# Three 256-column matmuls into one set of PSUM columns, in place of one of 512 and one of 256, in the feature blocks of a float32 decoder layer

## The chip, the core and the metric

One core of a Trainium2 chip. The metric is the device time of one execution in microseconds (us), the median of three runs. All times below are in us unless they are marked ns.

## What is computed

A hybrid decoder layer over 256 tokens and 2048 features, in float32: a recurrence with gates and a sparse attention side by side, merged, then a gated feed-forward part (ConvFFN), each followed by a layer norm. Cut to what the change touches:

```python
h = x @ w_in                                   # 2048 -> 12368 features
xr, gr, q, k, v, qi, ki, wi, g_rnn, g_att = split(h)
y_rnn = rg_lru(conv4(xr), ...) * gelu(gr)
score = sum_h wi_h * relu(rope(qi_h) @ rope(ki).T)   # top 64 keys of a query
y_att = attention(rope(q), rope(k), v, top-64 of score)
merged = sigmoid(g_rnn) * y_rnn + sigmoid(g_att) * y_att
x = layer_norm(2**0.25 * x + merged @ w_out)
u = conv3(x @ w_up)                            # 2048 -> 11264 features
x = layer_norm(2**0.25 * x + (silu(u[:, :5632]) * u[:, 5632:]) @ w_down)
```

## The kernel before, in words

**Splitting.** Every float32 operand of a product is split into a high part (cast to the type float32r) and a low part (the rest), and a product is the sum of three: high by high, high by low and low by high. A weight tile of 128 x 2048 is loaded by SyncE (SP), ScalarE (ACT) casts its two halves into `hi` (L116), VectorE (DVE) subtracts to get `lo` (L119). There are two `hi` and two `lo` buffers for each of two tiles, so the half of a tile can be cast when the same half of the tile two before it has left TensorE (PE). Casts and subtractions have priority over other work in the scheduler that orders each engine's queue.

**Feature blocks** (`feature_block`, L161). A block makes 128 output features (on partitions) for all 256 tokens (free). The source, `xt` or later `x1t` in the same place, holds for each of 16 groups of 128 input features 256 columns of high parts and then 256 columns of low parts. For each of the 16 groups, a *step* of the block, PE runs two matmuls: L170, the high weights by all 512 columns, into all 512 columns of the PSUM tile `psb`; and L174, the low weights by the 256 high columns, into the right half of `psb`. So the left half holds high by high, and the right half both cross terms. In the last step the order of the two is turned round.

**Evacuation** (`evacuate`, L311). ACT copies the right half of `psb` to a tile `ev` (L313), and DVE adds the left half to it and writes the destination (L314).

**Order of the work.** One block after another is written in program order; `project` (L185) runs a block, what takes its result, and then whatever was put off for some blocks (`after`, `tick`). The 181 feature blocks are: one for the indexer's key (80 features), 8 for its queries (`qi`), 4 for keys (`k`), 16 for queries (`q`) and 16 for the attention gate (`ga`), 48 for the recurrence (`xr`, `gr`, `gn`), and 88 for ConvFFN (L667). The products for values, `w_out` and `w_down` (`psv`, `pso`, `psd`) work the other way round, with tokens on partitions and matmuls of 512 columns throughout (`token_half`, L197 to L201).

**What stands between blocks.** Behind a `qi` block come the indexer's scores of an earlier block (`logits`, L383); behind `q` blocks the attention of one head (`attend`, L452 to L456, five matmuls of 256 columns, and `turn`, L475); behind `xr` blocks `gates` (L555 to L557, six matmuls of 256 columns: three add up in one half of a PSUM tile, three in the other). `k` and `q` results go through the rotation `rope` (shuffle on DVE L330, then three operations on GpSimd (POOL) L331 to L333) before ACT casts them. After the fourth `gn` block of a group ACT takes a sigmoid (L600), POOL a product and a sum (L601, L603), and ACT casts the merged result (L604).

Of the kernel before, what the change touches and what calls it, by code (L numbers as in the profile page):

```python
# [9 lines left out]
F32 = mybir.dt.float32  # L10
# [4 lines left out]
P = 128  # L15
PRIO = 30
T = 256
D = 2048
KT = D // P
# [7 lines left out]
LRU_C = 8.0  # L27
# [7 lines left out]

# Column starts in w_in.
C_XR, C_GR, C_Q, C_K, C_V, C_QI, C_KI, C_GRNN, C_GATT = (
    0, 2048, 4096, 6144, 6656, 7168, 8192, 8272, 10320)

# Columns of the per-feature parameters.  # L40
O_CW, O_CB, O_BA, O_BI, O_LAM, O_G1, O_B1, O_FW, O_FB = (
    0, 64, 80, 96, 112, 128, 144, 160, 424)
N_PAR = 512
# Columns of the constants.
O_ID, O_CI, O_SI, O_PEN = 0, 128, 384, 640
# [4 lines left out]
def hybrid_layer(ctx, tc, x, xT, w_blk, w_ki, w_v, lru_w, par, w_o, w_u, w_d, lnrows, consts, rot, out):  # L50
    nc = tc.nc
# [5 lines left out]

    # ---------------------------------------------------------------- weights
    order = []
# [34 lines left out]
    done = {"load": 0, "split": 0}  # L94
# [42 lines left out]

    # Work that is to wait until some more weight tiles have gone through the tensor engine.
    later = []
# [19 lines left out]

    # Features on partitions, tokens free: columns 0..255 hi*hi, 256..511 the cross terms.  # L160
    def feature_block(key, src, m=P):  # L161
        halves = weights(key)
        ps = psum.tile([P, 512], F32, tag="b", name="psb", bufs=4)
        for k in range(KT):
            hi, lo = halves[k // 8]
            o = (k % 8) * m
            first, last = k == 0, k == KT - 1

            def high():
                nc.tensor.matmul(ps[:m, :], hi[:, o:o + m], src[:, k, :], start=first, stop=last,  # L170
                                 skip_group_check=True)

            def low():
                nc.tensor.matmul(ps[:m, T:], lo[:, o:o + m], src[:, k, :T], start=False, stop=False,  # L174
                                 skip_group_check=True)
            if last:
                low()
                high()
            else:
                high()  # L180
                low()
        return ps

    # A block, its evacuation and then whatever waited for it.
    def project(key, fn, src=None, m=P):  # L185
        fn(feature_block(key, xt if src is None else src, m))
        tick()

    # Tokens on partitions, 512 features free; src_hi/src_lo hold features on partitions.
    def token_half(halves, t, ps, k0, hi_at, lo_at, kn):  # L190
# [19 lines left out]

    # The last tiles of a product: the first 128 tokens go through all of them, then the others.
    def token_tiles_held(keys, pss, k0, src, pool, between):
# [13 lines left out]
    nsp = base.tile([P, KT], F32, name="nsp")  # L226
# [6 lines left out]

    # Layer norm of the 128 rows r, 512 columns after another; done(c) takes them.
    def norm(r, g, b, t, done):
# [28 lines left out]

    # ---------------------------------------------------------------- phase 1
    wide = pool("wide")
# [13 lines left out]
    for k0, k1 in zip(cuts, cuts[1:]):  # L280
        r = xraw[k0 // 8][:, k0 % 8 * T:(k0 % 8 + k1 - k0) * T]
# [4 lines left out]
        r = r.rearrange("p (k t) -> p k t", t=T)  # L286
# [7 lines left out]
    for s in range(4):  # L294
        r = raw[:, s * 512:(s + 1) * 512]
        nc.sync.dma_start(r, order[1][1][:, s * 512:(s + 1) * 512])
        hi, lo = (h[:, s % 2 * 512:(s % 2 + 1) * 512] for h in halves[s // 2])
# [13 lines left out]
    def evacuate(ps, dst, work, m=P):  # L311
        t = work.tile([P, T], F32, tag="ev", name="ev", bufs=3)
        nc.scalar.copy(t[:m], ps[:m, T:])  # L313
        nc.vector.tensor_add(dst, ps[:m, :T], t[:m])  # L314

# [3 lines left out]

    # ---- indexer  # L320
    # Scores and attention weights keep queries 128..255 against all keys in columns 0..255,
    # queries 0..127 against keys 0..127 in columns 256..383.
    W2 = T + P
# [86 lines left out]

    # ---- keys and values
    # The parts of a key block lie side by side: keys 0..127 high, low, keys 128..255 high, low.
    kx = pa.tile([P, KV, 2, 2, P], F32R, name="kx")
# [23 lines left out]

    # ---- attention, one group of query heads after another
    def got_q(ps, n, g, pth, ptl):
# [66 lines left out]

    # ---- RG-LRU, four blocks of features at a time
    phm = ExitStack()
# [5 lines left out]

    # nsp = -LRU_C * softplus(-lambda), log1p by its series in e / (2 + e).
    lam = parm[:, O_LAM:O_LAM + KT]
# [47 lines left out]
    def recur(j0, v):  # L564
        xc, rg, ig, aa, th = (v[s] for s in ("xc", "rg", "ig", "aa", "th"))
        for i in range(NB):
            nc.scalar.activation(th[:, i], rg[:, i], AF.Tanh, scale=nsp[:, j0 + i:j0 + i + 1])
        for i in range(NB):
            nc.scalar.activation(aa[:, i], rg[:, i], AF.Exp, scale=nsp[:, j0 + i:j0 + i + 1])
        # 1 - a^2 = -tanh(log a) * (1 + a^2)  # L570
        nc.scalar.activation(rg, aa, AF.Square)
        nc.vector.scalar_tensor_tensor(th, rg, 1.0, th, op0=ALU.add, op1=ALU.mult)
        nc.scalar.activation(th, th, AF.Sqrt, scale=-1.0)
        nc.vector.tensor_mul(ig, ig, xc)
        nc.vector.tensor_mul(ig, ig, th)
        for i in range(NB):
            nc.vector.tensor_tensor_scan(rg[:, i], aa[:, i], ig[:, i], 0.0, op0=ALU.mult, op1=ALU.add)
# [30 lines left out]

    # ---------------------------------------------------------------- w_out and the first norm
    pho = ExitStack()  # L610
# [46 lines left out]

    # ---------------------------------------------------------------- ConvFFN
    phf = ExitStack()
# [27 lines left out]

    # ---------------------------------------------------------------- w_down and the second norm
    phd = ExitStack()
# [29 lines left out]
def _constants():  # L719
    def angles(rd):  # L720
        half = rd // 2
        inv = np.power(THETA, -np.arange(half, dtype=np.float64) * 2.0 / rd).astype(np.float32)
        ang = np.arange(T, dtype=np.float32)[:, None] * inv[None, :]
        return np.cos(ang.astype(np.float64)).T, np.sin(ang.astype(np.float64)).T

    c = np.zeros((P, N_CONST), np.float32)
    c[:, O_ID:O_ID + P] = np.eye(P)
    cos, sin = angles(16)
    c[:, O_CI:O_CI + T] = 1.0
    for r in (0, 64):  # L730
        c[r:r + 8, O_CI:O_CI + T] = cos
        c[r + 8:r + 16, O_CI:O_CI + T] = cos
        c[r:r + 8, O_SI:O_SI + T] = -sin
        c[r + 8:r + 16, O_SI:O_SI + T] = sin
    cos, sin = angles(32)
    rot = np.zeros((32, 2 * T), np.float32)
    rot[:16, :T], rot[16:, :T] = cos, cos
    rot[:16, T:], rot[16:, T:] = -sin, sin
    # Queries 128..255 against all keys, then queries 0..127 against keys 0..127.
    q = np.arange(P)[:, None]  # L740
    c[:, O_PEN:O_PEN + T] = np.where(np.arange(T)[None, :] > q + P, CAUSAL_FILL, 0.0)
    c[:, O_PEN + T:O_PEN + T + P] = np.where(np.arange(P)[None, :] > q, CAUSAL_FILL, 0.0)
    return c, rot
# [62 lines left out]
```

## Time and profile before

| | |
|---|---|
| three runs | 1472.03, 1469.31, 1472.29; median 1472.03 |
| profiled execution: span from first to last instruction | 1469.3 |
| its own time: the run of that length | 1469.31 |
| PE busy | 1430.9 (97%), 7718 matmuls and as many weight loads |
| DVE, ACT, POOL busy | 1008.9 (69%), 760.5 (52%), 269.3 (18%) |
| share of feature-block matmuls in the chain that ended last | L170 44%, L174 22% |

How to read it: the span of the profiled execution is the time of the fastest of the three runs, and 2.7 below the median. A matmul's row says when it started and how long it took from end to end; matmuls overlap, so a row of 256 columns lasts 280 ns and the next starts 120 ns after it. What a matmul costs in a stream is therefore read from the starts of consecutive rows, not from durations or from the busy time. A weight load (PEld) has its own row, which overlaps the matmul before.

### The profile page before, as it was taken

The numbers are of one execution on the slowest core, as the hardware profiler recorded it, in microseconds if no ns is written. First come the engines' busy times: TensorE is split into PE (matmuls) and PEld (weight loads), VectorE is DVE, ScalarE is ACT, GpSimd is POOL, SyncE is SP. The second block draws the span as 40 slices with busy tenths as digits, with TensorE's granted clock in tenths as the row PEclk, the third lists the DMA queues.
The fourth block names the chain that finished last, engine by engine and source line by source line (L and its number), as shares of the span: only waits on it lengthen the run. The fifth ranks groups of instructions, "written<-read, shape, count | busy, mean of one in ns | idle before, by whom it ended". The sixth has DMA issues, their size and how long they took to land.

```text
span 1469.3 us, 19909 instructions
## 1 busy us (share of the span) xinstructions
PE 1430.9 (97%) x7718; PEld 1222.6 (83%) x7718; DVE 1008.9 (69%) x1462; ACT 760.5 (52%) x1068; POOL 269.3 (18%) x227
## 2 busy tenths in 40 slices
PE   7989999999999999999799999999999999999996
PEld 6868888888888888888688888888888888888885
DVE  5787766777777777665776777677767775545456
ACT  4444555568777777644344444444444444433342
POOL 3541122220020211110422112211221120000002
PEclk9999999999999999999899999999999999999998
DMA  7435544545545454576355555555555557555552
GB/s 270 161 135 192 180 142 168 186 164 194 203 155 215 143 201 152 192 300 215 143 190 183 183 190 190 183 182 191 189 185 182 191 188 272 206 207 198 190 199 86
DMA packets 42205, 275.41 MB, mean 187 GB/s; under 512 B 4576, under 2 KB 4832, under 8 KB 10240
## 3 DMA queue, kind: packets, MB, share of 16 engines
q1 hardware_dynamic: 42112, 274.16, 52.2%
q8 instruction: 60, 0.98, 0.3%
q14 instruction: 33, 0.27, 0.1%
HBM read 269.94 MB, written 4.19 MB: 187 GB/s over the span
## 4 chain that ended last, share of the span: by engine, by line
PE 91%; DVE 4%; POOL 2%; DMA 1%; issue 1%; ACT 0%; SPq 0%; ACTq 0%; POOLq 0%; DVEq 0%
PE psb L170 44%; PE psb L174 22%; PE psd L201 5%; PE psd L197 5%; PE psd L199 5%; PE pso L201 2%; PE pso L199 2%; PE pso L197 2%; DVE lo L119 1%; DMA cst<-in_consts 1%; POOL qf L333 0%; POOL sh L332 0%; DMA xraw<-in_xT 0%; DVE rg L247 0%; PE psv L199 0%
## 5 line engine op out<-in xcount | busy, mean ns | idle before, releaser
L170 PE MATMUL psb<-xt,hi 128*128 128x512 f32 (+1 forms) x2896 | 1022.7, 400 | 6.4 <-ACT hi L116 5.4
L119 DVE TENSOR_TENSOR lo<-raw,hi 128x1024 fp32r<-128x1024 f32 (+2 forms) x488 | 609.9, 1253 | 361.7 <-ACT hi L116 352.1
L174 PE MATMUL psb<-xt,lo 128*128 128x256 f32 (+1 forms) x2896 | 786.1, 282 | 1.5 <-DVE lo L119 1.3
L116 ACT CAST hi<-raw 128x1024 fp32r<-128x1024 f32 (+1 forms) x488 | 509.5, 1048 | 365.8 <-PE psd L201 126.9
L170 PEld LDWEIGHTS psb<-xt,hi 128*128 128x128 f32 (+1 forms) x2896 | 536.8, 188 | 125.2 <-ACT hi L116 5.4
L174 PEld LDWEIGHTS psb<-xt,lo 128*128 128x128 f32 (+1 forms) x2896 | 547.9, 189 | 18.8 <-DVE lo L119 3.5
L683 POOL TENSOR_TENSOR y<-y 128x256 f32<-128x256 f32 x44 | 68.1, 1549 | 383.8 <-DVE y L675 362.3
L197 PE MATMUL psd<-hi,fh 128*128 128x512 f32 x352 | 136.9, 389 | 0.0
L199 PE MATMUL psd<-lo,fh 128*128 128x512 f32 x352 | 136.9, 389 | 0.0
L201 PE MATMUL psd<-hi,fl 128*128 128x512 f32 x352 | 136.9, 389 | 0.0
L675 DVE SCALAR_TENSOR_TENSOR y<-u,parm,y 128x255 f32<-128x255 f32 (+1 forms) x176 | 85.1, 484 | 6.2
L199 PEld LDWEIGHTS psd<-lo,fh 128*128 128x128 f32 x352 | 66.1, 188 | 13.8
L201 PEld LDWEIGHTS psd<-hi,fl 128*128 128x128 f32 x352 | 66.1, 188 | 13.7
L197 PEld LDWEIGHTS psd<-hi,fh 128*128 128x128 f32 x352 | 66.1, 188 | 13.5
L313 ACT COPY ev<-psb 128x256 f32<-128x256 f32 (+1 forms) x181 | 65.6, 362 | 0.8 <-PE psb L170 0.8
L684 ACT CAST fh<-y 128x256 fp32r<-128x256 f32 x44 | 17.9, 407 | 90.8 <-POOL y L683 90.8
L238 POOL TENSOR_SCALAR rstd<-mv 128x1 f32<-128x1 f32 x4 | 3.1, 778 | 294.8 <-DVE mv L236 294.8
L199 PE MATMUL pso<-lo,mh 128*128 128x512 f32 x128 | 49.9, 390 | 0.0
L197 PE MATMUL pso<-hi,mh 128*128 128x512 f32 x128 | 49.9, 390 | 0.0
L201 PE MATMUL pso<-hi,ml 128*128 128x512 f32 x128 | 49.8, 389 | 0.0
L331 POOL TENSOR_TENSOR qf<-qf,rots 32x256 f32<-32x256 f32 x16 | 15.5, 971 | 151.6 <-DVE sh L330 151.6
L681 ACT ACTIVATE y<-y 128x256 f32<-128x256 f32 x44 | 18.4, 419 | 47.0 <-DVE y L675 47.0
(172 smaller groups left out, 1028.0 us busy)
## 6 DMA issues: line engine op xcount, KB each, us to landing
raw<-in_w_blk SPq DMA_DIRECT2D x91, 1024.0 KB, 4.8
raw<-in_w_u SPq DMA_DIRECT2D x88, 1024.0 KB, 4.7
raw<-in_w_d SPq DMA_DIRECT2D x44, 1024.0 KB, 4.7
raw<-in_w_o SPq DMA_DIRECT2D x16, 1024.0 KB, 4.8
raw<-in_w_v SPq DMA_DIRECT2D x4, 1024.0 KB, 4.8
lwr<-in_lru_w SPq DMA_DIRECT2D x4, 512.0 KB, 3.7
g<-in_lnrows SPq DMA_DIRECT2D x2, 1024.0 KB, 6.6
xres<-in_x SPq DMA_DIRECT2D x4, 512.0 KB, 7.3
```

The lines of the kernel that those rows point to most:

```text
L116: nc.scalar.copy(hi[:, :w], raw[:, s * w:(s + 1) * w])
L119: eng.tensor_sub(lo[:, o:o + step], raw[:, s * w + o:s * w + o + step], hi[:, o:o + step].bitcast(F32))
L170: nc.tensor.matmul(ps[:m, :], hi[:, o:o + m], src[:, k, :], start=first, stop=last, skip_group_check=True)
L174: nc.tensor.matmul(ps[:m, T:], lo[:, o:o + m], src[:, k, :T], start=False, stop=False, skip_group_check=True)
L197: nc.tensor.matmul(ps, hi_at(k, t), hi[:, o:o + 512], start=first, stop=False, skip_group_check=True)
L199: nc.tensor.matmul(ps, hi_at(k, t), lo[:, o:o + 512], start=False, stop=False, skip_group_check=True)
L201: nc.tensor.matmul(ps, lo_at(k, t), hi[:, o:o + 512], start=False, stop=last, skip_group_check=True)
L313: nc.scalar.copy(t[:m], ps[:m, T:])
L675: nc.vector.scalar_tensor_tensor(y[:, s:], u[:, :T - s], w(tap), y[:, s:], op0=ALU.mult, op1=ALU.add)
L681: nc.scalar.activation(yg, yg, AF.Silu)
L683: nc.gpsimd.tensor_mul(yg, yg, yu)
L684: nc.scalar.copy(fh[:, j], yg)
```

## The change

A step of a feature block becomes three matmuls of 256 columns, all of which add up in the left half of `psb`: high weights by high columns, high weights by low columns, low weights by high columns. Every step has the same order, the last too. The evacuation becomes one ACT copy of that half straight to the destination; the tile `ev` and the DVE addition are gone. The rest of the diff removes comments. Line numbers after L164 fall by 12, from L314 on by 14.

```diff
         for k in range(KT):
             hi, lo = halves[k // 8]
             o = (k % 8) * m
-            first, last = k == 0, k == KT - 1
-
-            def high():
-                nc.tensor.matmul(ps[:m, :], hi[:, o:o + m], src[:, k, :], start=first, stop=last,
-                                 skip_group_check=True)
-
-            def low():
-                nc.tensor.matmul(ps[:m, T:], lo[:, o:o + m], src[:, k, :T], start=False, stop=False,
-                                 skip_group_check=True)
-            if last:
-                low()
-                high()
-            else:
-                high()
-                low()
+            hi, lo = hi[:, o:o + m], lo[:, o:o + m]
+            for n, (w, x) in enumerate(((hi, src[:, k, :T]), (hi, src[:, k, T:]), (lo, src[:, k, :T]))):
+                nc.tensor.matmul(ps[:m, :T], w, x, start=k == 0 and n == 0, stop=k == KT - 1 and n == 2)
         return ps
...
     def evacuate(ps, dst, work, m=P):
-        t = work.tile([P, T], F32, tag="ev", name="ev", bufs=3)
-        nc.scalar.copy(t[:m], ps[:m, T:])
-        nc.vector.tensor_add(dst, ps[:m, :T], t[:m])
+        nc.scalar.copy(dst, ps[:m, :T])
```

On PE, the first half of the first `qi` block, before (`hi_0`, `lo_0` are the first halves of its weight tile):

```order
L170 MATMUL psb<-xt,hi_0_115 128x512
L174 MATMUL psb<-xt,lo_0_116 128x256
L170 MATMUL psb<-xt,hi_0_115 128x512
L174 MATMUL psb<-xt,lo_0_116 128x256
L170 MATMUL psb<-xt,hi_0_115 128x512
L174 MATMUL psb<-xt,lo_0_116 128x256
```

and the same place with the change (x2: two such rows one after the other):

```order
L169 MATMUL psb<-xt,hi_0_115 128x256 x2
L169 MATMUL psb<-xt,lo_0_116 128x256
L169 MATMUL psb<-xt,hi_0_115 128x256 x2
L169 MATMUL psb<-xt,lo_0_116 128x256
L169 MATMUL psb<-xt,hi_0_115 128x256 x2
L169 MATMUL psb<-xt,lo_0_116 128x256
```

Two matmuls of a step have become three, for the same 768 columns.

On ACT, where the recurrence's first group of four ends and the next begins, before (`hi_0`, `hi_1`: the halves of one weight tile; `gn`: the gate's results; `mh`: the cast merged result; the brackets say which engines the row waits for):

```order
L313 COPY ev<-psb 128x256
L116 CAST hi_0_4077<-raw_3922 128x1024 [waits DMAHW1_49,DVE_49,PE_49]
L600 ACT_TABLE_LOAD
L600 ACTIVATE gn<-gn 128x1024 [waits DVE_49]
L116 CAST hi_1_4081<-raw_3922 128x1024 [waits PE_49,Activation_49]
L313 COPY ev<-psb 128x256
L604 CAST mh<-gn 128x1024 [waits Pool_49]
L116 CAST hi_0_4130<-raw_3968 128x1024 [waits DMAHW2_49,PE_49,Activation_49]
```

and with the change:

```order
L300 COPY gn<-psb 128x256 [waits PE_49]
L586 ACT_TABLE_LOAD
L586 ACTIVATE gn<-gn 128x1024 [waits Activation_49]
L116 CAST hi_0_4889<-raw_4692 128x1024 [waits DMAHW1_49,DVE_49,PE_49]
L590 CAST mh<-gn 128x1024 [waits Pool_49]
L116 CAST hi_1_4893<-raw_4692 128x1024 [waits DVE_49,PE_49]
L300 COPY xr<-psb 128x256 [waits PE_49]
L116 CAST hi_0_4956<-raw_4752 128x1024 [waits DMAHW2_49,DVE_49,PE_49]
```

The sigmoid has moved ahead of the first cast of the tile, and the cast of `mh`, which waits for POOL, now stands ahead of the second half of that tile and of the copy of the first `xr` block.

## Rows read from the trace of the kernel before

**Rows 1.** The page: PE's busy time, and the chain that ended last by engine and by line.

```profile
PE 1430.9 (97%) x7718; PEld 1222.6 (83%) x7718; DVE 1008.9 (69%) x1462; ACT 760.5 (52%) x1068; POOL 269.3 (18%) x227
PE 91%; DVE 4%; POOL 2%; DMA 1%; issue 1%; ACT 0%; SPq 0%; ACTq 0%; POOLq 0%; DVEq 0%
```

**Rows 2.** The page's groups of instructions: the two matmuls of a step (busy us, mean ns of one, idle before them).

```profile
L170 PE MATMUL psb<-xt,hi 128*128 128x512 f32 (+1 forms) x2896 | 1022.7, 400 | 6.4 <-ACT hi L116 5.4
L174 PE MATMUL psb<-xt,lo 128*128 128x256 f32 (+1 forms) x2896 | 786.1, 282 | 1.5 <-DVE lo L119 1.3
```

**Rows 3.** The chain in order of time: the last matmul of a ConvFFN block, and of the block 84 blocks later (start, us).

```profile
737.34 0.47 PE psb L170 x2
...
1212.22 0.47 PE psb L170 x2
```

**Rows 4.** Timeline of PE around one group of gates: start, us, line, shape.

```profile
363.70 0.39 PE L170 MATMUL psb<-xt,hi 128*128 128x512 f32 x1
363.93 0.28 PE L555 MATMUL pg<-xh,lwh 128*128 128x256 f32 x1
364.04 0.28 PE L556 MATMUL pg<-xl,lwh 128*128 128x256 f32 x1
364.16 0.28 PE L557 MATMUL pg<-xh,lwl 128*128 128x256 f32 x1
...
364.52 0.28 PE L557 MATMUL pg<-xh,lwl 128*128 128x256 f32 x1
364.64 0.40 PE L170 MATMUL psb<-xt,hi 128*128 128x512 f32 x1
364.87 0.28 PE L174 MATMUL psb<-xt,lo 128*128 128x256 f32 x1
```

**Rows 5.** Timeline of PE at one attention head: the first of its five matmuls of 256 columns (L452 to L456), and the matmul behind the fifth.

```profile
141.28 0.28 PE L452 MATMUL ps_s<-kx,qh 128*128 128x256 f32 x1
...
141.88 0.39 PE L170 MATMUL psb<-xt,hi 128*128 128x512 f32 x1
```

**Rows 6.** Timeline of PE in w_down, where all matmuls have 512 columns: nine matmuls from the first row to the last.

```profile
1299.78 0.39 PE L199 MATMUL psd<-lo,fh 128*128 128x512 f32 x1
...
1301.82 0.39 PE L199 MATMUL psd<-lo,fh 128*128 128x512 f32 x1
```

**Rows 7.** The chain in order of time: two starts of L170, nine steps apart, in a `qi` block right behind the indexer's scores.

```profile
42.86 0.23 PE psb L170
...
45.98 0.23 PE psb L170
```

**Rows 8.** Weight loads at the same gates, and the loads of two matmuls that follow each other with the same weights in w_down (L197, L199).

```profile
363.93 0.19 PEld L556 LDWEIGHTS pg<-xl,lwh 128*128 128x128 f32 x1
364.05 0.19 PEld L557 LDWEIGHTS pg<-xh,lwl 128*128 128x128 f32 x1
...
L199 PEld LDWEIGHTS psd<-lo,fh 128*128 128x128 f32 x352 | 66.1, 188 | 13.8
L197 PEld LDWEIGHTS psd<-hi,fh 128*128 128x128 f32 x352 | 66.1, 188 | 13.5
```

**Rows 9.** Groups: the addition that goes, in ConvFFN, the copy that stays, and the subtraction that makes `lo`.

```profile
L314 DVE TENSOR_TENSOR u<-psb,ev 128x256 f32<-128x256 f32 x88 | 36.8, 418 | 0.0
L313 ACT COPY ev<-psb 128x256 f32<-128x256 f32 x180 | 65.2, 362 | 0.8 <-PE psb L170 0.8
...
L119 DVE TENSOR_TENSOR lo<-raw,hi 128x1024 fp32r<-128x1024 f32 (+2 forms) x488 | 609.9, 1253 | 361.7 <-ACT hi L116 352.1
```

**Rows 10.** Groups of PE by shape whose idle time another engine ended: values, indexer scores, gates.

```profile
L199 PE MATMUL psv<-lo,xt 128*128 128x512 f32 x32 | 13.5, 422 | 3.5 <-DVE lo L119 3.5
L556 PE MATMUL pg<-xl,lwh 128*128 128x256 f32 x32 | 9.3, 292 | 2.0 <-DVE xl L547 2.0
L555 PE MATMUL pg<-xh,lwh 128*128 128x256 f32 x32 | 9.3, 290 | 1.7 <-ACT xh L546 1.7
L383 PE MATMUL pl<-kih,qil 64*128 64x256 f32 x32 | 4.9, 300 | 0.9 <-POOL qil L372 0.9
```

**Rows 11.** Busy time by stretch, for the key blocks and the value product that follows: length, busy us (x instructions) of PE, PEld, DVE, ACT and POOL, then PE's granted clock as a share of full speed, the DMA share, and GB/s.

```profile
95.00:108.00 13.00, 9.21 (x40) 6.52 (x39) 11.14 (x34) 5.14 (x8) 3.63 (x4) 1.00 0.28 105
108.00:115.00 7.00, 7.00 (x24) 5.58 (x25) 7.00 (x25) 3.36 (x4) 2.14 (x3) 0.76 0.48 159
```

**Rows 12.** Timelines of ACT and POOL where the first group of the recurrence ends, and from the chain the end of the second block behind that group.

```profile
399.66 0.36 ACT L313 COPY ev<-psb 128x256 f32<-128x256 f32 x1
...
402.47 1.28 ACT L600 ACT_TABLE_LOAD   x1
403.76 1.06 ACT L600 ACTIVATE gn<-gn 128x1024 f32<-128x1024 f32 x1
...
410.67 1.05 ACT L604 CAST mh<-gn 128x1024 fp32r<-128x1024 f32 x1 [4.63 <-POOL gn L603]
...
404.90 2.40 POOL L601 TENSOR_TENSOR gn<-gn,rg 128x1024 f32<-128x1024 f32 x1 [20.12 <-ACT gn L600]
407.38 3.25 POOL L603 TENSOR_TENSOR gn<-gn,macc 128x1024 f32<-128x1024 f32 x1
...
409.73 0.47 PE psb L170 x2
```

## The prediction

> **What bounds the kernel now.** I read the page first. PE is busy 97% of the span, and 91% of the chain that ended last is PE [rows 1]. The two matmuls of a feature block's step are the costliest groups, 2896 steps in 181 blocks, and PE hardly idles ahead of them: 6.4 and 1.5 us in all [rows 2]. So the stream of matmuls sets the time, and the question is how far apart they start. Durations do not tell: a row of 256 columns lasts 282 ns [rows 2], yet starts come closer. From the end of one ConvFFN block to the end of the one 84 blocks later it is 1212.22 - 737.34 = 474.88 us [rows 3], so a block takes 5.653 us and a step, with 768 columns, 353.3 ns. Almost all blocks run so.
>
> Three other places show what a matmul costs in a stream. The clock is granted in full nearly everywhere, 1.00 in the first row of [rows 11], the level of 2.4 GHz, at which 512 columns last 213.3 ns and 256 last 106.7. In w_down nine matmuls of 512 columns take 1301.82 - 1299.78 = 2.04 us, 226.7 ns each [rows 6]: 13.3 over their columns. At an attention head five of 256 take 0.60 us, 120 ns each [rows 5]: again 13.3 over. Around the gates, two of 512 and six of 256 take 364.87 - 363.70 = 1.17 us; their 2560 columns are 1066.7 ns, which leaves 12.9 ns for each of the eight [rows 4]. One price fits all three: **the columns, and some 13.3 ns for each matmul whatever its width**. By that price a step of before would take 226.7 + 120 = 346.7 ns. Some blocks do: behind the indexer's scores nine steps take 3.12 us, 346.7 each [rows 7]. The common 353.3 is 6.7 ns more, a loss of the alternating stream that I can't explain from the rows.
>
> **The change, part by part.**
>
> *A step has three matmuls.* The columns stay at 768, and one more price of 13.3 ns comes in. The gates and the head are the nearest rows, since they are the new stream in small: matmuls of 256 columns, three in a row into the same PSUM columns, two of them with the same weights. I take 120 ns each, the head's value, so 360 ns a step and 16 x 360 = 5.760 us a block, 0.107 more than now. Over 181 blocks that is **+19.3 us**. Blocks that now run at 346.7 lose another 0.107. I estimate 28 of them, those behind the gates (16 groups of them, two of the 32 rows L555 in each [rows 10]) and about as many behind other inserted matmuls: **+3.0 us**.
>
> The bounds of this price: from below, the six matmuls of the gates start 364.64 - 363.93 = 0.71 us from end to end, 118.3 ns each [rows 4], a step of 355.0, +4.8 us over 181 blocks. I take that as the low end and not the likely value, because the two matmuls of 512 around them start 230 ns before the next, and give the 3 ns back: it is where the start is marked that differs. From above, the new stream could also lose 6.7 ns a step, as the old one does: 366.7, +38.6 us.
>
> The Trainium skill, in "TensorE: Matmul & The Clock Gate", section "Back-to-back issue gap", gives the gap between matmuls at full clock as the columns over 2.4 plus some 2.5 ns. By that the split would cost 2.5 ns a step, 2896 x 2.5 = 7.2 us. The trace does not agree: it shows 13.3 [rows 5, 6].
>
> *Weight loads.* Each matmul has its own load, also where two in a row have the same weights: L197 and L199 have 352 loads each [rows 8]. So 2896 loads are added, not shared. At the gates a load starts every 120 ns or so, with the start of the matmul before it, and the matmuls keep their pace [rows 4, 8]. I cost them at nothing, covered by a matmul of 256 columns; the cover is shorter than half of what a 512 gives. Without it, the case above of 366.7 is my price.
>
> *The evacuation.* 181 additions on DVE go, 0.418 us each in ConvFFN [rows 9], some 75 us off an engine that does not bound. The ACT copy of 0.362 [rows 9] stays, with another destination. In ConvFFN and the recurrence PE runs on beside all that, so it is worth nothing there. It is worth something where PE waited for a chain through the addition. In the key blocks copy, addition, shuffle, POOL's rotation and ACT's cast follow each other, and DVE is 11.14 busy of 13 us [rows 11]; PE waits 3.5 us for DVE at the values [rows 10]. Four key blocks with 0.418 less each: -1.7. The scores wait 0.9 for POOL's low part of the query, behind the same chain [rows 10], in waits of about the addition's length: -0.9. Together **-2.6 us**. At most, both waits go, those of the gates go too (2.0 + 1.7), and the clock, granted at 0.76 over 7 us after PE had been busy only 9.21 of 13 us [rows 11], stays at 1.00: 3.5 + 0.9 + 3.7 + 7 x 0.24 = 9.8 us. At least, nothing.
>
> *The order of ACT's queue.* Where a group of the recurrence ends, the cast of `mh` now stands ahead of the second half of a weight tile. In before it came 410.67 - 404.82 = 5.85 us after the sigmoid's end, since POOL's product and sum take 2.40 and 3.25 us [rows 12]. What queues behind it is that half, its subtraction on DVE, and PE through that. But the sigmoid itself has moved ahead of a cast: its table load can start at 400.0, when the last copy of `gn` ends, and not at 402.47 [rows 12]. So `mh` comes 2.4 earlier, near 408.2, the half is cast by 410.3 and subtracted, in 1.25 us [rows 9], by 411.6. PE needs it half a block, 2.8 us, behind the block's start at about 409.8 [rows 12], at 412.6. I cost it at nothing; without the cover, one subtraction late at three such places is +3.8. The gates that follow wait for DVE and ACT as before.
>
> **The sum**: 19.3 + 3.0 - 2.6 = +19.7 us, so 1469.3 + 19.7 = 1489.0 for the profiled execution. Its time is its span, and the median of the three runs is 2.7 above it, so I predict **1491** for the median, 1.3% slower.
>
> **The rivals.**
>
> *The relief decides (faster).* Place: the key blocks and the ends of the recurrence's groups. If a matmul takes 118.3 ns in the long stream, PE loses only 4.8 us, and if the shorter chains take away most of the waits, 9.8 come back: 1472.0 + 4.8 - 9.8 = 1467. It decides from the point where a step is under about 353.3 + 9.8 us / 2896 = 356.7 ns. For it: the starts at the gates, and that the DVE queue is full just there. Against it: the head's 120, and the whole relief is needed. Chance 0.17.
>
> *A small price for one matmul more.* The 6.7 ns that the alternating stream loses would go with the alternation, and all but 2.5 of the extra 13.3 would be covered in the same way: a step of 355.8, +7.2 - 2.6, 1476.6. This is also where the rule of the Trainium skill would lead. For it: steps of two kinds exist already [rows 3, 7]. Against it: no place of 256 columns shows so low a price. Chance 0.08.
>
> *The loss stays.* The new stream settles 6.7 ns a step above its parts, as the old does, because the next weights have less time: 366.7 ns, +38.6 - 2.6, 1508. For it: 353.3 is the rule and 346.7 the exception. Against it: five and six in a row show no such loss. Chance 0.12.
>
> *It does not do what it says.* If the second of two matmuls with the same weights needed no load and ran on as one of 512, a step would be 346.7 and the time 1472 - 19.2 - 2.6 = 1450. Against it: the loads of L197 and L199. Chance 0.03.
>
> The forecast has what is left, 0.60.
>
> **How the numbers follow.** A measurement of this kernel tells a change of about 0.2%, 2.9 us, from none. The forecast's own bounds, with the relief between 0 and 9.8, the 3.0 of the quick blocks doubtful and the late casts between 0 and 3.8, are 1482 to 1498. The range goes down to the faster rival's 1467, and up to 1504, a part of the way to the lost 6.7: **1467 to 1504**. It leaves out most of the 1508 case, the 1450 case, and the lower half of the faster one. Faster: 0.16, the two faster cases without those that end near 1470. Same: 0.08, the upper part of the relief case and the lower part of the small price. Slower: 0.76.
>
> **What the new profile would show.** Starts of the step's matmuls 120 ns apart, and a ConvFFN block of 5.76 us; 5.69 or less would make the forecast wrong, 5.87 the loss. PE with 10614 matmuls and as many loads, busy still near 97%. DVE busy near 933 us, without the addition. The wait at the values shorter than 3.5 us, those at the gates about as now. A PE that idles for DVE or ACT at the recurrence's ends for more than 4 us would show that the queue order was mis-costed.

## The result, and the profile after

The changed kernel takes **1489.04 us** (median of 4 executions, 1488.78 to 1490.25) against 1471.72 of the kernel before beside it (4 executions, 1469.31 to 1472.29). The ratio is 1.0122, with a 95% interval of 1.0108 to 1.0136: slower by 1.2%. The profiled execution took 1490.25 us with a span of 1488.5, so that the spans of the two traces differ by 1488.5 - 1469.3 = 19.2 us, and the medians by 17.3. The granted clock is 0.990 in the mean, 0.991 before. In every execution for which both are known, the time is 1.7 to 2.5 us longer than the span; so the execution profiled before, with its span of 1469.3, lasted some 1471 us by this (an estimate), and then was not the one of 1469.31.

The page of after: busy time of the engines, and the shares of the chain that ended last, as in [rows 1].

```profile
PE 1452.9 (98%) x10614; PEld 1382.4 (93%) x10614; DVE 958.7 (64%) x1281; ACT 762.7 (51%) x1068; POOL 241.8 (16%) x227
PE 91%; DVE 4%; POOL 2%; DMA 1%; ACT 1%; issue 1%; SPq 0%; POOLq 0%; ACTq 0%; DVEq 0%
```

PE has 10614 matmuls and 10614 loads, 2896 more of each, and DVE has its 181 additions less. Nothing else came to bound the kernel: the chain is PE's to 91% as before.

The groups of a step, which answer to [rows 2], and the subtraction of [rows 9] (busy us, mean ns of one, idle before them).

```profile
L169 PE MATMUL psb<-xt,hi 128*128 128x256 f32 (+1 forms) x5792 | 1054.0, 285 | 8.5 <-ACT hi L116 7.3
L169 PE MATMUL psb<-xt,lo 128*128 128x256 f32 (+1 forms) x2896 | 822.7, 284 | 1.4 <-DVE lo L119 1.3
L119 DVE TENSOR_TENSOR lo<-raw,hi 128x1024 fp32r<-128x1024 f32 (+2 forms) x488 | 627.9, 1291 | 432.7 <-ACT hi L116 416.3
```

The idle time ahead of the steps is 2 us more (8.5 + 1.4 us, 6.4 + 1.5 before). What grew is how long the stream itself takes. The timeline of PE in ConvFFN (start, us) shows how it runs; a row with x2 holds two matmuls.

```profile
999.90 0.28 PE L169 MATMUL psb<-xt,lo 128*128 128x256 f32 x1
1000.02 0.40 PE L169 MATMUL psb<-xt,hi 128*128 128x256 f32 x2
1000.26 0.28 PE L169 MATMUL psb<-xt,lo 128*128 128x256 f32 x1
1000.38 0.40 PE L169 MATMUL psb<-xt,hi 128*128 128x256 f32 x2
...
1001.34 0.28 PE L169 MATMUL psb<-xt,lo 128*128 128x256 f32 x1
```

From one low product to the next it is 0.36 us, and from 999.90 to 1001.34 four steps take 1.44: 360 ns a step, 120 a matmul. Over a long stretch it is the same, here of L169 alone (length, busy us and instructions of PE and PEld, granted clock, DMA share, GB/s).

```profile
740.00:1220.00 480.00, 480.00 (x4003) 480.00 (x4002) 1.00 0.53 184
```

480 us / 4003 is 119.9 ns, and 48 of these make a block of 5.76 us, against 5.653 in [rows 3].

Not every stage lost. By the same markers in both traces (first and last instructions of a stage), after is 6.2 us late where the first indexer scores begin, has 0.9 of it back at the first value product and 5.1 more within that product, and stands 0.1 us late when the values are done, at 124.6 us. The 19.0 us that are missing at the end all come behind that point, where 168 of the 181 blocks lie: 0.113 us a block. Of these 19.0, 1.6 fall in the product w_out, which the change leaves as it was: 3.4 us of it run at half clock in this trace (from 713.8 us) and none in that of before. Traces of kernels whose blocks behind the values are those of before have this stretch too, so it is not the change's; without it, it is 0.104 us a block. So the early part holds two effects that nearly cancel. The first is a gain at the values and a shorter wait there, which the groups by shape show beside the gates and scores, as in [rows 10].

```profile
L187 PE MATMUL psv<-lo,xt 128*128 128x512 f32 x32 | 12.6, 394 | 1.0 <-DVE lo L119 1.0
L541 PE MATMUL pg<-xh,lwh 128*128 128x256 f32 x32 | 9.3, 292 | 0.7 <-ACT xh L532 0.7
L542 PE MATMUL pg<-xl,lwh 128*128 128x256 f32 x32 | 9.3, 290 | 2.0 <-DVE xl L533 2.0
L369 PE MATMUL pl<-kih,qil 64*128 64x256 f32 x32 | 4.5, 280 | 0.0
```

The second is a loss of some 6 us near 30 us, which the prediction did not have. It stands in the timelines of ACT and of PE of after (idle before an instruction, and what ended it, in brackets).

```profile
26.56 0.37 ACT L300 COPY qf<-psb 128x256 f32<-128x256 f32 x1
30.03 0.40 ACT L357 CAST qih<-qf 128x256 fp32r<-128x256 f32 x1 [3.09 <-POOL qf L319]
...
29.18 0.29 PE L345 MATMUL pw<-ident,kw 16*128 16x16 f32 x2
31.43 0.79 PE L169 MATMUL psb<-xt,hi 128*128 128x256 f32 x2 [1.96 <-ACT hi L116]
32.69 0.58 PE L169 MATMUL psb<-xt,lo 128*128 128x256 f32 x1 [0.47 <-DVE lo L119]
33.07 0.63 PE L169 MATMUL psb<-xt,hi 128*128 128x256 f32 x2
33.50 0.41 PE L169 MATMUL psb<-xt,lo 128*128 128x256 f32 x1
33.71 0.63 PE L169 MATMUL psb<-xt,hi 128*128 128x256 f32 x2
```

In ACT's queue the cast of the query, `qih`, now stands directly behind the copy, and ahead of the casts of the next weight tile. It waits 3.09 us for POOL, and the weights queue behind it. Before, they came ahead of it, right after the copy:

```profile
25.33 0.37 ACT L313 COPY ev<-psb 128x256 f32<-128x256 f32 x1
25.60 2.00 ACT L116 CAST hi<-raw 128x1024 fp32r<-128x1024 f32 x2
```

They start at 30.34 now. PE idles 1.96 us for them and then once more for DVE. Its clock falls within the first wait, at 31.16 us, and stays down for 6.8 us. The windows of after, with the columns of [rows 11]:

```profile
31.00:38.00 7.00, 6.10 (x27) 5.81 (x28) 5.61 (x7) 3.49 (x5) 3.83 (x4) 0.51 0.45 149
95.00:108.00 13.00, 13.00 (x84) 11.85 (x83) 11.94 (x42) 4.77 (x7) 3.02 (x3) 1.00 0.28 95
108.00:115.00 7.00, 6.00 (x27) 4.49 (x25) 5.90 (x21) 4.21 (x5) 2.15 (x3) 1.00 0.44 150
```

The first row is the price: seven microseconds at the level of 1.2 GHz. The other two show the gain: PE is busy for all of the 13 us, where [rows 11] had 9.21, and the clock stays at 1.00 behind them, where it had been 0.76. The two do not hold the same work, though: the value product begins at 101.3 us here and at 96.0 in before. From its first matmul to its last it takes 23.3 us, 28.5 before. A part of these 5.1 us is no gain of the shorter chain: PE comes 5.3 us later, and so waits less for `lo`. A kernel below that comes without the delay takes 25.2.

### The profile page after: what moved, and what is told of

Read it like the earlier page. It is cut to its first block, busy times and chain, and to the rows that moved or that the text cites. A ratio compares the mean times of both kernels' runs of the same rounds, so it can differ in the third digit from the quotient of the medians.

```text
span 1488.5 us, 25495 instructions
## 1 busy us (share of the span) xinstructions
PE 1452.9 (98%) x10614; PEld 1382.4 (93%) x10614; DVE 958.7 (64%) x1281; ACT 762.7 (51%) x1068; POOL 241.8 (16%) x227
## 4 chain that ended last, share of the span: by engine, by line
PE 91%; DVE 4%; POOL 2%; DMA 1%; ACT 1%; issue 1%; SPq 0%; POOLq 0%; ACTq 0%; DVEq 0%
PE psb L169 66%; PE psd L189 5%; PE psd L187 5%; PE psd L185 5%; PE pso L189 2%; PE pso L187 2%; PE pso L185 2%; DVE lo L119 2%; DMA cst<-in_consts 1%; DMA xraw<-in_xT 1%; ACT hi L116 0%; POOL sh L318 0%; DVE rg L235 0%; DVE r L235 0%; PE pl L369 0%
## 5 line engine op out<-in xcount | busy, mean ns | idle before, releaser
L169 PE MATMUL psb<-xt,hi 128*128 128x256 f32 (+1 forms) x5792 | 1054.0, 285 | 8.5 <-ACT hi L116 7.3
L169 PEld LDWEIGHTS psb<-xt,hi 128*128 128x128 f32 (+1 forms) x5792 | 907.2, 193 | 11.7 <-ACT hi L116 7.4
L119 DVE TENSOR_TENSOR lo<-raw,hi 128x1024 fp32r<-128x1024 f32 (+2 forms) x488 | 627.9, 1291 | 432.7 <-ACT hi L116 416.3
L169 PE MATMUL psb<-xt,lo 128*128 128x256 f32 (+1 forms) x2896 | 822.7, 284 | 1.4 <-DVE lo L119 1.3
L169 PEld LDWEIGHTS psb<-xt,lo 128*128 128x128 f32 (+1 forms) x2896 | 557.5, 193 | 2.4 <-DVE lo L119 2.3
L669 POOL TENSOR_TENSOR y<-y 128x256 f32<-128x256 f32 x44 | 33.4, 760 | 409.5 <-DVE y L661 381.3
L671 POOL TENSOR_TENSOR fl<-y,fh 128x256 fp32r<-128x256 f32 x44 | 50.4, 1145 | 22.7 <-ACT fh L670 22.7
L317 POOL TENSOR_TENSOR qf<-qf,rots 32x256 f32<-32x256 f32 x16 | 11.7, 729 | 153.7 <-DVE sh L316 153.7
L658 DVE TENSOR_SCALAR y<-u,parm 128x256 f32<-128x256 f32 x88 | 35.9, 408 | 0.0
```

What stands on the lines that cost most here:

```text
L119: eng.tensor_sub(lo[:, o:o + step], raw[:, s * w + o:s * w + o + step], hi[:, o:o + step].bitcast(F32))
L169: nc.tensor.matmul(ps[:m, :T], w, x, start=k == 0 and n == 0, stop=k == KT - 1 and n == 2)
L317: nc.gpsimd.tensor_mul(v, v, cos)
L658: nc.vector.tensor_scalar(y, u, w(2), parm[:, O_FB + j:O_FB + j + 1], op0=ALU.mult, op1=ALU.add)
L669: nc.gpsimd.tensor_mul(yg, yg, yu)
L671: nc.gpsimd.tensor_sub(fl[:, j], yg, fh[:, j].bitcast(F32))
```

## The experiments

Times are medians of several executions unless said otherwise; the ratio is to the kernel before, run beside it on the same chip. Where stages are compared, it is between one trace of each kernel, and a stage with the same code differs by up to 2 us between traces.

**The split alone.** The layout, the copy and the addition of before; only the 512 columns run as two matmuls of 256 from the second step of a block on.

```diff
-                nc.tensor.matmul(ps[:m, :], hi[:, o:o + m], src[:, k, :], ...)
+                cuts = ((0, 2 * T),) if first else ((0, T), (T, 2 * T))
+                for c0, c1 in cuts:
+                    nc.tensor.matmul(ps[:m, c0:c1], hi[:, o:o + m], src[:, k, c0:c1], ...)
```

> The matmul split alone, with the PSUM layout, the `ev` copy and the DVE addition of before: from its second step on, each step's 512 columns are run as 256 and 256, into the two halves they had. Theory (some 13.3 ns for each matmul whatever its width): starts 120 ns apart, a step of 360 ns, a ConvFFN block of 5.76 us, and no relief, so before + 19 to 22 us: 1491 to 1494. Rival A (it is the adding up in the same columns that costs): here two of three matmuls go to other columns, so the block stays near 5.65 us and the time near 1472. Rival B (a small price, 2.5 ns): 1479.

Measured: 1488.25 us against 1470.03, ratio 1.0117 (1.0102 to 1.0132): 18.2 us more. So the split alone makes a loss of this size, and adding up in the same PSUM columns has no price that shows beside it. One of 16 steps is unsplit here; by the same price all 16 would cost some 19.4. A window of ConvFFN, and the waits at the gates and the scores (L557, L558 and L385 are L555, L556 and L383 of before):

```profile
740.00:1200.00 460.00, 460.00 (x3760) 456.27 (x3759) 325.41 (x481) 218.76 (x321) 93.15 (x80) 1.00 0.53 183
```

```profile
L558 PE MATMUL pg<-xl,lwh 128*128 128x256 f32 x32 | 9.3, 290 | 1.4 <-DVE xl L549 1.3
L557 PE MATMUL pg<-xh,lwh 128*128 128x256 f32 x32 | 9.2, 289 | 0.9 <-ACT xh L548 0.9
L385 PE MATMUL pl<-kih,qil 64*128 64x256 f32 x32 | 4.7, 292 | 0.2 <-POOL qil L374 0.2
```

460 us / 3760 = 122 ns a matmul, the 512 in each block's first step included. The waits at the gates and the scores are 0.9 + 1.4 and 0.2 us, against 1.7 + 2.0 and 0.9 in [rows 10], although the addition is still there. So a slower stream shortens these waits by itself.

**Cut at 384 instead of 256.** The same number of matmuls and columns, but one of the three has only 128.

```diff
-                cuts = ((0, 2 * T),) if first else ((0, T), (T, 2 * T))
+                cuts = ((0, 2 * T),) if first else ((0, 384), (384, 2 * T))
```

> As the split alone, but the 512 columns are run as 384 and 128, so that there are again three matmuls for 768 columns. Theory that only the number of matmuls counts: 173 + 67 + 120 + ... = the same 360 ns a step and the same 1491 to 1494. Rival (a weight load of about 109 ns, the distance of the 128-column transposes, needs a matmul over it; 256 columns cover it and 128 don't): the matmul behind the 128 columns starts about 109 and not 67 ns after it, some 42 ns a step over 15 of 16 steps, 2715 x 0.042 = 115 us more, near 1608.

Measured: 1609.81 us, ratio 1.0947 (1.0930 to 1.0963), 139.8 more. The number of matmuls alone does not set the price: from the end of w_out to the end of ConvFFN this kernel loses 68.0 us to the 7.2 of the split at 256, which is (68.0 - 7.2) / (88 x 15) = 46 ns a step. PE's timeline of this kernel (a row of L172 with x2 is the 384 and the 128 behind it):

```profile
1000.74 0.28 PE L176 MATMUL psb<-xt,lo 128*128 128x256 f32 x1
1000.86 0.40 PE L172 MATMUL psb<-xt,hi 128*128 128x384 f32 x2
1001.10 0.33 PE L176 MATMUL psb<-xt,lo 128*128 128x256 f32 x1
1001.26 0.34 PE L172 MATMUL psb<-xt,hi 128*128 128x384 f32 x1
```

From one 384 to the next it is 0.40 us, not 0.36. The loss is marked behind the low product, 0.16 to the next start and not 0.12. It fits a weight load of about 110 ns that a matmul of 128 columns, 66.7 ns by the price of 13.3, is too short to cover: 43 ns a step are missing. Three matmuls of 256 do cover it, just. That it is the load, and not the short matmul itself, the next kernel shows.

**Six matmuls of 128 columns a step.** From the second step on, to see the load's own period.

```diff
+                cuts = ((0, 2 * T),) if first else tuple((c, c + P) for c in range(0, 2 * T, P))
...
+                for c in (0, P):
+                    nc.tensor.matmul(ps[:m, T + c:T + c + P], lo[:, o:o + m], src[:, k, c:c + P], ...)
```

> Six matmuls of 128 columns a step (four for the high weights, two for the low), from the second step of a block on, with the layout and the evacuation of before; the columns are still 768. By 13.3 ns a matmul alone: 6 x 66.7 = 400 ns a step, 2715 x 0.0467 = 127 us over before, 1597. If a weight load of about 109 ns binds: 6 x 109 = 654, 2715 x 0.301 = 817 us over before, 2287, and the distance of the starts is the load's period.

One execution: 3177.27 us, beyond both numbers. Two windows of it, at full and at half clock, and PE's timeline in each:

```profile
600.00:1100.00 500.00, 500.00 (x4209) 489.77 (x4209) 210.62 (x244) 210.47 (x267) 36.71 (x15) 1.00 0.34 116
1200.00:2900.00 1700.00, 1700.00 (x7887) 1691.85 (x7886) 351.97 (x508) 234.38 (x338) 62.83 (x86) 0.50 0.15 53
```

```profile
999.82 0.61 PE L172 MATMUL psb<-xt,hi 128*128 128x128 f32 x4
1000.26 0.38 PE L177 MATMUL psb<-xt,lo 128*128 128x128 f32 x2
...
1499.62 1.05 PE L172 MATMUL psb<-xt,hi 128*128 128x128 f32 x4
1500.47 0.63 PE L177 MATMUL psb<-xt,lo 128*128 128x128 f32 x2
```

At full clock four matmuls take 0.44 us: 110 ns each, 111 in the mean of the long stretch, though their columns last 53. Whether the load or the matmul itself sets this pace is told by the first block, the indexer's key, whose weights have 80 columns and not 128. Its rows, at half clock and then at full clock (granted from 17.5 us on):

```profile
13.46 0.73 PE L172 MATMUL psb<-xt,hi 128*80 128x128 f32 x4
13.99 0.47 PE L177 MATMUL psb<-xt,lo 128*80 128x128 f32 x2
...
17.90 0.45 PE L172 MATMUL psb<-xt,hi 128*80 128x128 f32 x4
18.19 0.31 PE L177 MATMUL psb<-xt,lo 128*80 128x128 f32 x2
```

The matmuls have the same 128 columns, but start 0.53 / 4 = 133 ns apart and then 0.29 / 4 = 72, where with 128 weight columns it is 213 and 111. Both ratios are near 80 / 128. So the pace follows the weights: it is the load's period, as at the cut at 384. The expectation had not seen the clock: from 1150.7 us to 2925.6 it is granted at 0.50, and a matmul then takes 0.85 / 4 = 213 ns. It fell in a wait of PE of 5.1 us between w_out and ConvFFN, stayed down while PE was busy all through ConvFFN, and rose 4.4 us after the 512-column matmuls of w_down had begun. Both the load and the clock make this kernel slow.

**The evacuation alone.** The matmuls of before; the copy goes straight to its destination and the addition is gone. The cross terms are left out of the sum.

```diff
     def evacuate(ps, dst, work, m=P):
-        t = work.tile([P, T], F32, tag="ev", name="ev", bufs=3)
-        nc.scalar.copy(t[:m], ps[:m, T:])
-        nc.vector.tensor_add(dst, ps[:m, :T], t[:m])
+        nc.scalar.copy(dst, ps[:m, :T])
```

> The evacuation alone: matmuls of 512 and 256 as before, and one ACT copy of the left half in place of copy and addition, so the cross terms are left out of the result. Theory: in the changed kernel the order of ACT's queue costs 6.2 us at the second query block (PE idle, then at half clock) and the shorter chains give back about 6 until the values are done, 1.4 at the gates; the sum of both is near zero, so 1470 to 1473, with the same half clock near 30 us. Rival (the relief counts, the loss at 30 us comes from the slower matmuls): 1465 or less and no half clock near 30 us.

Measured: 1465.44 us, ratio 0.9965 (0.9951 to 0.9979), 4.6 less, and not the 1470 to 1473 of the expectation. The relief is larger than the 2.6 of the sum. By stages it is late by 4.5 us at the first scores, and 2.0 ahead at the end of the values; the recurrence gives 3.4. The wait of ACT's queue is there too (3.08 us before `qih`), without any change in the matmuls, so the order makes it, and not the split; the half clock is shorter here, 3.4 us. The gains of this kernel and the loss of the split do not simply add up: 18.2 - 4.6 = 13.6, where the whole change costs 17.3. Its window, and its gates and values by shape:

```profile
31.00:38.00 7.00, 6.24 (x25) 5.15 (x26) 5.49 (x7) 3.03 (x5) 4.03 (x3) 0.76 0.44 164
```

```profile
L553 PE MATMUL pg<-xh,lwh 128*128 128x256 f32 x32 | 9.0, 281 | 0.0
L199 PE MATMUL psv<-lo,xt 128*128 128x512 f32 x32 | 12.8, 401 | 1.1 <-DVE lo L119 1.1
```

**The first query cast on POOL.** The changed kernel, with the one cast that holds up ACT's queue moved off it.

```diff
-        nc.scalar.copy(qh, qf)
+        (nc.gpsimd.tensor_copy if i == 0 else nc.scalar.copy)(qh, qf)
```

> The changed kernel with one instruction moved: the cast of the first query block's high part is done by POOL and not by ACT, so that it no longer stands ahead of the next weight casts in ACT's queue. Theory (this cast makes PE idle 2.6 us and then run 6.8 us at half clock, 6.2 us in all): no half clock near 31 us, 1489 - 6 = 1483. Rival (the key blocks are bound by their own chain through DVE and POOL, and what PE gains ahead of them it waits there): the values' waits grow by as much, 1486 to 1489.

Measured: 1487.09 us, ratio 1.0108 (1.0093 to 1.0123), which overlaps the changed kernel's own interval. Its windows and its values:

```profile
31.00:38.00 7.00, 7.00 (x63) 6.73 (x63) 4.94 (x6) 1.33 (x3) 6.26 (x7) 1.00 0.54 178
95.00:112.00 17.00, 14.62 (x69) 11.47 (x69) 14.83 (x53) 5.92 (x9) 5.18 (x6) 1.00 0.37 125
```

```profile
L187 PE MATMUL psv<-lo,xt 128*128 128x512 f32 x32 | 12.8, 400 | 2.4 <-DVE lo L119 2.4
```

The cause of the stall is confirmed: the seven microseconds run at full clock, and the first scores are reached 4.8 us earlier than in the changed kernel. But much of it is handed back. PE comes earlier to the values, is busy 14.62 us in these 17 and not 17.00, and waits 2.4 us there and not 1.0. The values are done 2.5 us earlier than in before. Of the profiled executions this one is 2.9 us shorter than the changed kernel's; the ratios do not tell them apart.

**Where the 353.3 ns come from: two orders of a step.** The kernel before swaps the two matmuls in a block's last step. One kernel never swaps, the other swaps in every step but the first.

```diff
-            if last:
+            if not first:
                 low()
                 high()
```

> The kernel before, with the last step of a block in the same order as the others (512 columns, then 256), so that 512 and 256 alternate over block ends too; the sum is the same. The common step of before is 353.3 ns, 6.7 above its two parts of 226.7 and 120; blocks at 346.7 turn into blocks at 353.3 where two matmuls of 512 follow each other, at a block's end. Theory (that meeting of two of 512 starts the loss): blocks stay at 5.55 us, 150 blocks x 0.107 = 16 us less, near 1454. Rival (the loss is the alternation's own): a block of 5.65 us, 1470 to 1472.

> The kernel before with the order turned round in all steps but the first (256 columns, then 512), so that two of 256 meet at the end of the first step and two of 512 at the end of a block. Theory (a meeting of equals shifts the stream into the loss): as before, 353 ns a step, 1470 to 1473. Rival (the order within a step decides, and the weights of a 512 need the time under a 512): more than 2 us of difference to before.

Measured: without the swap 1470.93 us, ratio 0.9986 (0.9967 to 1.0005); with it everywhere 1469.39, ratio 0.9989 (0.9979 to 0.9999). Neither differs by more than 2 us. Counted from the start of a block's first matmul to that of its 29th, 14 steps later, the kernel before has 143 blocks at 352 to 354 ns a step and 16 at 347 or 348. No swap has 153 and 3, in a trace of its slowest execution, and all swapped has 155 and 7; the remaining blocks hold a wait or lie beyond these values. The 6.7 ns thus belong to the alternation of 512 and 256 in either order; why, these two do not tell.

**The change in 13 blocks only.** The kernel before, with the three matmuls and the single copy in the indexer's key block, its eight query blocks and the four key blocks, and the query cast on POOL as above. Everything behind keeps the alternating pair.

```diff
+            if (key if key == "ki" else key[0]) in FOLD:    # FOLD = ('ki', 'qi', 'k')
+                hi, lo = hi[:, o:o + m], lo[:, o:o + m]
+                for n, (w, x) in enumerate(((hi, src[:, k, :T]), (hi, src[:, k, T:]), (lo, src[:, k, :T]))):
+                    nc.tensor.matmul(ps[:m, :T], w, x, start=first and n == 0, stop=last and n == 2)
+                continue
```

> The kernel before, with the change made in the first 13 blocks alone (indexer key and queries, keys), where a chain through DVE's addition holds PE up, and with POOL casting the first query block. All other blocks keep 512 and 256 columns. Theory (the evacuation is worth something only here): the price is 13 x 0.107 = 1.4 us, and the end of the value product comes 2.5 us earlier than in before, as in the changed kernel with the moved cast; nothing else changes, so before - 2.5. Rival (the relief of the whole change lies in the recurrence): no difference to before.

Measured: 1468.05 us against 1470.79, ratio 0.9979 (0.9970 to 0.9987): 2.7 less, faster than both kernels by a little. Its windows:

```profile
31.00:38.00 7.00, 7.00 (x64) 6.73 (x63) 4.49 (x6) 1.34 (x3) 6.32 (x6) 1.00 0.60 199
108.00:115.00 7.00, 6.01 (x26) 4.42 (x25) 6.85 (x14) 4.08 (x6) 0.00 (x0) 1.00 0.44 158
```

Both stretches run at full clock. In the trace the value product ends 2.9 us earlier than in the kernel before: the 13 blocks pay 13 x 0.107 = 1.4 us for their matmuls and have more than that back in the shorter chain. The gates wait 1.7 + 1.9 us as before; their blocks kept both the addition and the pace of before.

**The change in the four key blocks only.** The same with `FOLD = ('k',)` and no cast moved.

> The kernel before, with the change made in the four key blocks alone. Theory (the chain of the key blocks is shorter by an addition each): 4 x 0.107 = 0.4 us more for PE, 4 x 0.42 = 1.7 less in the chain, and the half clock of 3.4 us near 108 us goes if PE's idle time gets short enough, another 1.7: before - 1.3 to - 3. Rival (the chain of the query blocks hands its lateness on): no difference.

Measured: 1472.43 us, ratio 1.0011 (1.0002 to 1.0020): no gain, a miss. The clock behind the key blocks does stay at 1.00, but the values wait longer than ever:

```profile
108.00:115.00 7.00, 4.79 (x19) 3.54 (x20) 5.89 (x22) 3.14 (x4) 2.16 (x3) 1.00 0.41 150
```

```profile
L205 PE MATMUL psv<-lo,xt 128*128 128x512 f32 x32 | 12.9, 404 | 5.3 <-DVE lo L120 5.3
```

PE comes to the values no earlier (at 97.0 us, 96.0 in before), runs them at full clock, and `lo` is not there. It is DVE's subtractions that set the pace there, and the time moved from the clock into the wait. So the addition in the key blocks was not by itself what held this place back, as the prediction had it. Which of the other blocks of the 13, or the cast on POOL, gives the gain was not tried apart.

## Why the prediction was right

1491 us was forecast and 1489.04 measured, 1489.0 for the span and 1488.5. The main term, the price of a third matmul, is what the runs show. That the rest of the sum fits as well is partly luck: the 3.0 was high, and the -2.6 stands for a larger relief and a loss that was not foreseen. The 2.7 from span to median rests on a misreading of the time of the profiled execution; by the 1.7 to 2.5 above it should have been about 2.

**The price of a matmul.** The step that carries the sum holds: 120 ns a matmul, 360 a step, 5.76 us a block, each as forecast. The split alone makes 18.2 us. By the sum's two terms, 15 of 16 steps split should have cost 15/16 x (19.3 + 3.0) = 20.9; behind the values the changed kernel pays 0.104 us a block where the two terms together have 22.3 / 181 = 0.123. The two terms are right within about 15%. The estimate of 28 quick blocks looks high: 16 of 16 + 143 are at the quick pace, which makes 18 blocks and 1.9 us. What the sum also left out is that a slower PE waits less: at the gates and the scores these waits are 2.1 us shorter with the split alone.

**The low end and the small price.** The starts at the gates [rows 4] had given 118.3; in the long stream it is 120, so the head's value was the one to take. The rival of a small price, 1476.6, is refuted by both kernels that split at 256: 13.3 ns over the columns is what each shows. The Trainium skill, in "TensorE: Matmul & The Clock Gate", section "Back-to-back issue gap", gives some 2.5 ns over the columns at full clock, for a matmul by itself; by this the split would have cost 7.2 us, as an estimate. The traces do not agree.

**The loss that stays, and the shared load.** 366.7 ns a step did not come: three equal widths lose nothing. And the second matmul with the same weights does load again: 10614 loads for 10614 matmuls.

**Weight loads at nothing.** Right, but with a margin that the prediction did not know. It said that the cover is shorter than half of what a 512 gives, but 120 of 226.7 ns is a little more than half, and it left as the price without cover 6.7 ns a step. The runs at 128 columns show a period of 110 to 112 ns, so a matmul of 256 covers its load with 8 to 10 ns to spare. Where one load in a step is not covered, as in the cut at 384, the price is not 6.7 but 46 ns a step.

**The evacuation.** This term, -2.6, was mis-sized, in two parts that nearly cancelled. The relief up to the end of the values is larger. The two kernels without the stall near 30 us are done there 2.5 and 2.9 us ahead of before, and have paid 13 x 0.107 = 1.4 for their blocks: a relief of some 4. The half clock behind the key blocks, which stood only in the upper bound, went, and the wait at the values fell from 3.5 to 2.4. Against it stands the loss near 30 us. The prediction took "another destination" for the copy as no change, and asked what stands behind the moved casts only at the ends of the recurrence's groups. The same kind of move happened in the second query block, where the cast waits for POOL with a weight tile behind it: 6.2 us with the clock, of which the values, now reached late, take back a part. In the changed kernel, gain and loss leave 0.1 us at 124.6 us, the price of the 13 blocks included. The split alone and the whole change, 1.0117 and 1.0122, cannot be told apart; with the split of all 16 steps at 19.4, the net of this term comes to some 2 us, and with these intervals it may also be nothing. So that the forecast has about the right net is luck.

**ACT's queue at the recurrence's ends.** At nothing, and so it is: the gates wait 0.7 + 2.0 us, 1.7 + 2.0 before, and PE idles only 8.5 + 1.4 us ahead of all steps, the stall near 30 us among them. The test of over 4 us at the recurrence's ends was not met. But that the evacuation is worth nothing in the recurrence, as the prediction had it, holds only at the new pace. With the old pace, the evacuation alone takes both waits at the gates away altogether, and the recurrence is 3.4 us quicker. At 120 ns a matmul it is 4.2 slower, where the split alone, with the addition, is 3.2 slower: no relief shows there.

**DVE.** 958.7 us and not the 933 that was forecast. The additions went, but the subtractions take 1291 ns and not 1253, 627.9 us and not 609.9, which is 18 of the 26 us; why they take longer was not tried. Since DVE does not bound, it cost nothing that these runs show.

**The faster rival** needed a step under 356.7 ns. The relief that it spoke of is real, and in 13 blocks with the queue mended it is worth 2.7 us; over 181 blocks it can't pay for 360.

## What to carry to other kernels

In a stream that PE bounds, count matmuls beside columns: a split that adds no column still costs what a trace shows between starts, here 13.3 ns each, and below the width that covers a weight load, here near 256 columns, it costs far more. A shorter chain on other engines is worth having only in the stretch where PE waits for that chain, so apply such a change there, keep the wide matmul elsewhere, and measure it: in 13 blocks it gave 2.7 us, in four of them nothing. And when an instruction disappears from one engine, look at every place in the in-order queues where a neighbour may now stand ahead of something that PE needs, not only where the change looks large.

## What the runs showed of the hardware that was not expected

- The load of 128 x 128 weights has a period of its own of 110 to 112 ns at full clock and 213 at half clock, and matmuls of 128 columns, whose columns last 53 ns at full clock, run at that pace. With 80 weight columns it is 72 and 133.
- At the level of 1.2 GHz the extra price of a matmul does not show: near 33 us in the changed kernel a step of three takes 33.71 - 33.07 = 0.64 us, which is its 768 columns at that clock.
- With 128-column matmuls the clock was granted at 0.50 for 1775 us (1150.7 to 2925.6) although PE was busy 100% in the records. It had been at 1.00 for the same stream before it fell in a wait of PE. Why it did not rise again stays open.
- A stream that alternates 512 and 256 columns loses 6.7 ns a step, in either order, where three times 256 loses nothing. The cause stays open too. The kernel without the swap scatters: its ten executions lie between 1462.46 and 1473.56 us, the kernel before between 1468.40 and 1472.81 beside it. A pace that settles one way or the other would make this, but that was not tried.
- A short idle of PE can cost more than itself: in a wait of 1.96 us for ACT the clock fell at 31.16 us, and 6.8 us ran at half clock. In the kernel with the moved cast, a wait of 0.44 us for DVE at the same place left it at 1.00.
